# Channel norms in a hybrid decoder layer: sums of split squares on two columns, and factor rows that go through DRAM

## The chip, the cores and the metric

The kernel runs on one core of a Trainium2 chip, as one launch. The metric is the device time of that launch in microseconds (us). The core's engines have one name each here: PE is TensorE (matmuls; PEld are its weight loads), DVE is VectorE, ACT is ScalarE, POOL is GpSimd, SP is SyncE. SP, POOL and ACT each have a queue of transfers.

## What is computed

One decoder layer on 512 tokens of width 1024, all in fp32: a SwiGLU feed-forward network (ffn1), a hybrid mixer (a Mamba-2 scan of four groups and differential attention of eight heads, with one input and one output projection), cross attention into 256 memory tokens, a second feed-forward network (ffn2) and a last norm. The change touches two norms of the mixer. In the attention, the output of each head (128 channels) is normed for each token:

```python
w = p[:, :, 0] - lam * p[:, :, 1]
o = einsum('bhqk,bkhe->bqhe', w, v)          # 8 heads, 128 channels
...
o = o * lax.rsqrt(jnp.mean(o * o, axis=-1, keepdims=True) + EPS)
y_attn = (o * subln_w * (1.0 - lambda_init)).reshape(bsz, seqlen, DA_WIDTH)
```

In the scan, the gated output of each group (256 channels) is normed for each token:

```python
y = y.reshape(bsz, seqlen, SSD_WIDTH) * jax.nn.silu(z)
yg = y.reshape(bsz, seqlen, SSD_GROUPS, SSD_WIDTH // SSD_GROUPS)
yg = yg * lax.rsqrt(jnp.mean(yg * yg, axis=-1, keepdims=True) + EPS)
y_ssd = yg.reshape(bsz, seqlen, SSD_WIDTH) * ssd_norm_w
...
return jnp.concatenate([y_ssd, y_attn], axis=-1) @ w_out
```

## The kernel before

Everything is kept with channels on the 128 partitions and the 512 tokens along the row, so a projection takes its weights in blocks of 128x128 and 512 columns of tokens. Each fp32 matrix is split into a high and a low part of a type with which PE multiplies at full rate (fp32r, called `R32`), and a product is three passes: high by high, high by low, low by high. `split` (with `split_into`, lines 152 to 163) makes the parts: the high part by a copy on ACT (line 155), the low part by a subtraction on DVE (line 156). `mm` (lines 143 to 146) issues a matmul, `transpose` (148 to 150) a transpose on PE. Weights come through three buffers: `wr` is loaded by SP's or POOL's queue and split into `wh` and `wl`.

The stages follow one another on PE: ffn1 up to about 345 us, the mixer up to about 837, cross attention up to about 950, ffn2 to the end. In the mixer the dense work (projections `pq`, `pk`, `pv`, `pxbc`, `pz`, and blocks of the output projection `pm`) runs as one chain of generators, and the work of heads and groups is woven into it by the class `Order`. It counts PE's time as instructions are issued (`od.t`); a head or group is a chain that yields a delay from the table `W`, and its next step is issued into the program when the count has reached that point. The order on PE, DVE and ACT then follows from a scheduler that starts from this program order; POOL's and SP's instructions stay in program order. Accumulators for dense work have four banks of PSUM (`acc`), those of heads and groups four others (`aux`).

**A head** (`head`, from line 756) computes scores (`ps`), exponentials (`ec`), their combination, and transposes them (`pt`, `wt`). Then `po` is the product with `v`, channels on partitions, and `of` its copy in SBUF (line 844, ACT). The norm needs a sum over the channels, which lie on the partitions. The head turns `of` round by four transposes (`ptk`), so that tokens are on the partitions; squares and sums it in four passes of ACT (`junk`, line 852); adds the epsilon term (`ev`, DVE); takes the power −1/2 on POOL (`rr`, line 857); multiplies (`on`, line 859, DVE); and turns the result back by four transposes (`pot`). `ya` is the split of that with the norm's weights; the output projection `out_attn` reads it.

**A group** (`group`) multiplies its two halves by the gate, squares them (`ysq`, lines 1020 and 1022), and sums over the partitions with PE: `pn` takes the squares as weights, in blocks of 128x128, and a column of ones, so that four columns hold the sums with tokens on the partitions. This is an fp32 matmul, and the trace shows it as two records each. `inv_rms_cols` (lines 362 to 368) adds the epsilon (`nv`, DVE, line 365) and takes the power (`ncol`, POOL, line 367). `row_of` (lines 370 to 383) makes of these 128x4 factors a row of 512 on all partitions: it splits the factors (`ch`, `cl`, POOL), multiplies each with the identity matrix (two `ndiag`, POOL), and sums over the partitions with two matmuls (`nrow`). The two halves `y` are multiplied with it (line 1033, DVE) and split (`ys`).

Beside this, a generator sums weight blocks for ffn2 in DRAM all through the mixer (`block_sums_in_dram`, lines 1270 to 1292): SP copies a block (line 1285), and POOL's queue adds another to it by an accumulating transfer (line 1289; `isum`, `wsum`).

## Time and profile before

| what | value |
|---|---|
| time, median of 3 runs | 1294.87 us (1294.66 to 1296.31) |
| profiled execution | 1296.09 us, of which its span 1294.1 |
| PE busy | 1281.5 us, 99% of the span |
| PE weight loads | 1123.7 us, 87% |
| DVE busy | 971.9 us, 75% |
| ACT busy | 707.6 us, 55% |
| POOL busy | 118.0 us, 9% |
| mean share of the DMA engines | 42.2% by the queues that SP feeds, 19.9% by POOL's |

A row of a timeline has the start in us, the busy time in us, the engine, the line, the operation and `out<-in` by the program's names, with the tile's size; `x4` says that four like instructions are put into one row, and a bracket at the end has the idle time before it and what ended it. The busy times of neighbouring matmuls overlap a little, since they are pipelined: how long a burst takes is read from the starts of what stands before and behind it. A row of the windows has the stretch, its length, and the busy time and number of instructions of PE, PEld, DVE, ACT and POOL, then the granted clock, the share of the DMA engines and GB/s. A row of transfers has the KB of one and the median time from its issue to its landing.

### The profile page before, as it was taken

How to read it: one execution, taken by the hardware profiler on the slowest of the kernel's cores; microseconds unless marked ns; L12 is line 12 of the kernel's file. 1: busy time of each engine (PE TensorE's matmuls, PEld its weight loads, DVE VectorE, ACT ScalarE, POOL GpSimd, SP SyncE). 2: the span in 40 equal slices, each digit the busy share in tenths (PEclk: the TensorE clock that was granted, in tenths of full speed). 3: DMA queues.
4: the chain of work that ended last, by engine and by line, in shares of the span. 5: the costliest groups of instructions: out<-in, count | busy, mean ns of one | idle time of the engine just before them, and what ended most of it. 6: DMA issues, size and time to landing. Idle time of an engine off the chain costs nothing.

```text
span 1294.1 us, 20089 instructions
## 1 busy us (share of the span) xinstructions
PE 1281.5 (99%) x7709; PEld 1123.7 (87%) x7709; DVE 971.9 (75%) x1549; ACT 707.6 (55%) x1203; POOL 118.0 (9%) x149
## 2 busy tenths in 40 slices
PE   9999999999999999999999999999999999999997
PEld 7889998998988778877888888889899999989995
DVE  6988898797876686567868696645678868877886
ACT  7545564565654564447644574435466646555554
POOL 1001010001101011101102011020001000000000
PEclk9999999999999999999999999999999999999998
DMA  9368677788875436653476567593249876666662
GB/s 331 101 170 209 187 199 199 226 208 227 272 232 155 131 66 169 224 163 96 107 211 187 151 163 227 193 234 107 66 132 255 210 221 184 191 189 190 180 201 92
DMA packets 69551, 234.75 MB, mean 181 GB/s; under 512 B 8192, under 2 KB 9696, under 8 KB 69104
## 3 DMA queue, kind: packets, MB, share of 16 engines
q1 hardware_dynamic: 53488, 180.91, 42.2%
q0 software_dynamic: 13168, 45.67, 19.9%
q10 hardware_dynamic: 2800, 6.91, 1.7%
q8 instruction: 60, 0.98, 0.3%
q14 instruction: 35, 0.29, 0.1%
HBM read 231.30 MB, written 48.29 MB: 216 GB/s over the span
## 4 chain that ended last, share of the span: by engine, by line
PE 82%; issue 12%; DMA 2%; ACT 1%; DVE 1%; POOL 1%; POOLq 0%; SPq 0%; ACTq 0%
PE qb L243 12%; PE pm L146 10%; PE qe L243 8%; PE qa L243 8%; PE pxbc L146 5%; PE ob L1327 5%; PE oa L1327 4%; PE oe L1327 4%; PE pcq L146 3%; PE pz L146 3%; PE pa L146 2%; PE pk L146 2%; PE pq L146 2%; PE pcv L146 2%; PE pv L146 2%
## 5 line engine op out<-in xcount | busy, mean ns | idle before, releaser
L155 ACT ACTIVATE wh<-wr 128x1024 fp32r<-128x1024 f32 (+1 forms) x245 | 251.2, 1028 | 235.2 <-PE qe L243 27.9
L156 DVE TENSOR_TENSOR wl<-wr,wh 128x1024 fp32r<-128x1024 f32 (+1 forms) x245 | 290.8, 1188 | 83.5 <-ACT wh L155 61.3
L1313 ACT ACTIVATE wh<-wr 128x1024 fp32r<-128x1024 f32 (+1 forms) x78 | 76.9, 987 | 68.4 <-PE ob L1327 19.5
L1315 DVE TENSOR_TENSOR wl<-wr,wh 128x1024 fp32r<-128x1024 f32 (+1 forms) x78 | 87.5, 1131 | 15.0 <-ACT wh L1313 13.1
L789 ACT ACTIVATE ec<-ec,mn 128x512 f32<-128x512 f32 (+3 forms) x64 | 35.4, 554 | 21.9 <-DVE mn L788 21.9
L788 DVE CUSTOM_DVE_ANT_0 ec<-ps,bias 128x512 f32<-128x512 f32 (+3 forms) x64 | 28.1, 486 | 14.8 <-PE ps L146 14.7
L252 POOL DMA_DIRECT2D wr<-in_f2q x11 | 9.7, 881 | 309.8 <-DMA wr<-in_f2q 156.2
L902 DVE SCALAR_TENSOR_TENSOR conv<-pxbc,par,conv 128x511 f32<-128x511 f32 (+2 forms) x48 | 35.7, 745 | 2.3 <-ACT conv L898 1.5
L367 POOL TENSOR_TENSOR ncol<-nv,mhalf 128x4 f32<-128x4 f32 (+1 forms) x9 | 9.7, 1077 | 294.1 <-DVE nv L365 266.5
L146 PE MATMUL pxbc<-hnl,wh 128*128 128x512 f32 x128 | 35.4, 403 | 0.0
L146 PE MATMUL pxbc<-hnh,wh 128*128 128x512 f32 x128 | 35.3, 400 | 0.0
L146 PE MATMUL pxbc<-hnh,wl 128*128 128x512 f32 x128 | 32.3, 393 | 0.0
L454 DVE TENSOR_TENSOR gate<-qb,row 128x512 f32<-128x512 f32 x19 | 13.2, 692 | 22.1 <-PE qb L243 22.1
L146 PEld LDWEIGHTS pxbc<-hnh,wl 128*128 128x128 f32 x128 | 23.8, 188 | 5.3 <-issue 0.3
L252 POOL DMA_DIRECT2D wr<-in_f1q x16 | 14.0, 875 | 152.8 <-DMA wr<-in_f1q 49.8
L146 PEld LDWEIGHTS pxbc<-hnl,wh 128*128 128x128 f32 x128 | 23.3, 188 | 4.8 <-issue 0.4
L146 PEld LDWEIGHTS pxbc<-hnh,wh 128*128 128x128 f32 x128 | 23.2, 189 | 4.5 <-issue 0.3
L455 ACT ACTIVATE gate<-gate 128x1024 f32<-128x1024 f32 x19 | 20.1, 1056 | 10.9 <-DVE gate L454 10.9
L146 PE MATMUL pv<-wh,hnh 128*128 128x512 f32 x64 | 25.3, 395 | 0.0
L146 PE MATMUL pv<-wh,hnl 128*128 128x512 f32 x64 | 25.2, 393 | 0.0
L155 ACT ACTIVATE s24h<-s 128x512 fp32r<-128x512 f32 x30 | 18.8, 627 | 9.0 <-DVE s L214 8.9
L857 POOL TENSOR_TENSOR rr<-ev,mhalf 128x4 f32<-128x4 f32 x8 | 8.3, 1035 | 161.3 <-DVE ev L855 161.3
(465 smaller groups left out, 3546.9 us busy)
## 6 DMA issues: line engine op xcount, KB each, us to landing
wr<-in_f2q SPq DMA_DIRECT2D x44, 512.0 KB, 4.8
wr<-in_f1q SPq DMA_DIRECT2D x40, 512.0 KB, 4.5
wr<-in_f1b SPq DMA_DIRECT2D x23, 512.0 KB, 5.7
isum<-in_f2q SPq DMA_DIRECT2D x22, 512.0 KB, 5.8
wr<-isum SPq DMA_DIRECT2D x22, 512.0 KB, 4.0
wsum<-in_f2b SPq DMA_DIRECT2D x20, 512.0 KB, 6.3
wr<-wsum SPq DMA_DIRECT2D x20, 512.0 KB, 4.7
wr<-in_f1q POOLq DMA_DIRECT2D x16, 512.0 KB, 7.2
```

The source lines that it names most:

```text
L146: newest_mm[:] = [nc.tensor.matmul(out, w, x, start=start, stop=stop).ins]
L155: S.activation(hi, src, AF.Copy),
L156: V.tensor_tensor(lo, src, hi.bitcast(F32), ALU.subtract),
L243: newest_mm[:] = [nc.tensor.matmul(out, w_[:, wc], xs[kp][which][x_], start=first and j == 0 and f == 0 and kp == 0, stop=j == 2 and kp == ...
L252: last_sum[:] = [G.dma_start(raw, m, accum_op=ALU.add).ins]
L455: S.activation(gate, gate, AF.Silu)
L788: V.tensor_tensor_reduce(out=ec[:, :n], in0=ps[c][:, parts[i]], in1=bias[:, T - n :], scale=0.125, scalar=3e38, op0=ALU.add, op1=ALU.min, ...
L789: S.activation(ec[:, :n], ec[:, :n], AF.Exp, bias=mn, scale=-1.0, accum_out=sm[c][:, i : i + 1])
L902: V.scalar_tensor_tensor(y[:, d:], ps[:, : T - d], par[:, cw + j : cw + j + 1], y[:, d:], ALU.mult, ALU.add)
L1313: high = S.activation(hi, raw, AF.Copy)
L1315: low = V.tensor_tensor(lo, raw, hi.bitcast(F32), ALU.subtract)
L1327: newest_mm[:] = [nc.tensor.matmul(ps, a_[:, ts], b_[:, ws], start=first and k == 0 and j == 0, stop=k == n - 1 and j == 2, skip_group_che ...
```

## The change

Six of the eight heads (those with `hd % 4 < 3`: 0, 1, 2, 4, 5 and 6) take a new way, `normed_far`. The square of `of` is taken with channels on partitions (`osq`, ACT) and split into halves (`osqh` on ACT, `osql` on DVE). The sums come from PE as in the groups, with the halves of the squares as weights, but from fp32r matmuls on two columns of ones (`pon`, eight of them). `ev` and `rr` follow on DVE and POOL. The 128x4 factors are then written to DRAM (`there`) and read back on all partitions as a row of 512 (`far`), both by POOL's queue (`row_by_dram`, with the delays `rw` and `rr` of the table); DVE multiplies `of` with the weights and the row (`on`), which is read with a stride of four since the row in DRAM has the four blocks inmost; and `ya` is split from SBUF. The transposes `ptk` and `pot` and the passes `junk` are not done in these heads. Heads 3 and 7 keep the old way.

In all four groups the summed squares are split and `pn` is made of eight fp32r matmuls on two columns. Groups 0, 1 and 2 take `row_by_dram` in place of `row_of`; group 3 keeps `row_of`.

```diff
+W |= {"hn": 4.2, "rw": 8.0, "rr": 12.0}
...
+    def row_by_dram(col, landed, read):
+        there = dram.tile([P, 4], F32, name=nm("there"))
+        G.dma_start(there, col)
+        yield landed
+        row = s2("far")
+        G.dma_start(row, bass.AP(there.tensor, there.offset, [[0, P], [1, 4 * P]]))
+        yield read
+        return row.rearrange("p (t b) -> p b t", b=4)
+
+    def blocks(t):
+        return t.rearrange("p (b t) -> p b t", b=4)
...
         of = s2("of")
         S.activation(of, po, AF.Copy)
+        if hd % 4 < 3:
+            yield from normed_far(hd, of, sm[0])
+            return
         yield W["hv"]
         pt = aux("ptk")
...
+    def normed_far(hd, of, sums):
+        sq = s2("osq")
+        S.activation(sq, of, AF.Square)
+        sq = split("osq", sq)
+        yield W["hn"]
+        pon = aux("pon", (P, 4, 2))
+        for b in range(4):
+            for j in range(2):
+                mm(pon[:, b], sq[j][:, b * P : (b + 1) * P], ones_r[:, 0:2], j == 0, j == 1)
+        ev = small("ev", 4)
+        V.scalar_tensor_tensor(ev, sums, EPS, sums, ALU.mult, ALU.mult)
+        V.scalar_tensor_tensor(ev, pon[:, :, 0], 1.0 / P, ev, ALU.mult, ALU.add)
+        rr = small("rr", 4)
+        G.tensor_tensor(rr, ev, mhalf, ALU.pow)
+        row = yield from row_by_dram(rr, W["rw"], W["rr"])
+        on = s2("on")
+        V.scalar_tensor_tensor(blocks(on), blocks(of), wsub, row, ALU.mult, ALU.mult)
+        ya[hd] = split("ya", backwards(on))
         dump(f"ya_{hd}", ya[hd][0])
...
         V.tensor_tensor(sq[0], sq[0], sq[1], ALU.add)
+        sq = split("ysq", sq[0])
         yield W["gq"] + (1.2 if g == 2 else 0.0)
-        pn = aux("pn", (P, 4))
+        pn = aux("pn", (P, 4, 2))
         for b in range(4):
-            mm(pn[:, b : b + 1], sq[0][:, b * P : (b + 1) * P], ones[:, 0:1], True, True)
-
-        rh = inv_rms_cols(pn, 4, 4.0 / (4 * 256), 4.0 * EPS)
-        yield W["gn"]
-        pr = yield from row_of(rh, 4, G, G, W["gr"])
+            for j in range(2):
+                mm(pn[:, b], sq[j][:, b * P : (b + 1) * P], ones_r[:, 0:2], j == 0, j == 1)
+
+        rh = inv_rms_cols(pn[:, :, 0], 4, 4.0 / (4 * 256), 4.0 * EPS)
+        if g < 3:
+            pr = yield from row_by_dram(rh, W["rw"], W["rr"])
+        else:
+            yield W["gn"]
+            pr = blocks((yield from row_of(rh, 4, G, G, W["gr"])))
         for j in range(2):
             n = 2 * g + j
-            V.scalar_tensor_tensor(yz[j], yz[j], par[:, C_SSD + n : C_SSD + n + 1], pr, ALU.mult, ALU.mult)
+            V.scalar_tensor_tensor(blocks(yz[j]), blocks(yz[j]), par[:, C_SSD + n : C_SSD + n + 1], pr, ALU.mult, ALU.mult)
             ys[n] = split("ys", yz[j])
```

The change moves instructions. On PE in head 1 (the weights of a dense matmul are `wh` or `wl`, here of `pk`; a row names the moving operand first, and the number behind a name tells buffers apart), this stood there before, where a transpose of the head's next weights ends and the dense `pk` runs on:

```order
L150 MATMUL pt_4998<-ident,ec_4872 128x128
L150 MATMUL ptk_5003<-ident,of_4960 128x128 x4
L146 MATMUL pk_4930<-hnl_3919,wh_4933 128x512
L146 MATMUL pk_4930<-hnl_3947,wh_4933 128x512
L146 MATMUL pk_4930<-hnl_3969,wh_4933 128x512
L146 MATMUL pk_4930<-hnl_3999,wh_4933 128x512
L146 MATMUL pk_4930<-hnl_4027,wh_4933 128x512
L146 MATMUL pk_4930<-hnl_4047,wh_4933 128x512
L146 MATMUL pk_4930<-hnh_3870,wl_4934 128x512
L146 MATMUL pk_4930<-hnh_3888,wl_4934 128x512
L146 MATMUL pk_4930<-hnh_3918,wl_4934 128x512
```

And this stands there now, a few matmuls further on:

```order
L147 MATMUL pk_4933<-hnl_4047,wh_4936 128x512
L147 MATMUL pk_4933<-hnh_3870,wl_4937 128x512
L147 MATMUL pk_4933<-hnh_3888,wl_4937 128x512
L147 MATMUL pon_5020<-ones_r,osqh_4967 128x2
L147 MATMUL pon_5020<-ones_r,osql_4968 128x2
L147 MATMUL pon_5020<-ones_r,osqh_4967 128x2
L147 MATMUL pon_5020<-ones_r,osql_4968 128x2
L147 MATMUL pon_5020<-ones_r,osqh_4967 128x2
L147 MATMUL pon_5020<-ones_r,osql_4968 128x2
L147 MATMUL pon_5020<-ones_r,osqh_4967 128x2
L147 MATMUL pon_5020<-ones_r,osql_4968 128x2
L147 MATMUL pk_4933<-hnh_3918,wl_4937 128x512
```

The `ptk` burst behind `pt` is gone, and the `pon` burst stands eight dense matmuls later, behind the first two of the pass with `wl`.

On DVE at group 0 (`wl` are low parts of weights that `pv` and `pq` read, `nv` the epsilon step, `vl` the low part of a finished bank of `pv`), this stood there before:

```order
L365 TENSOR_SCALAR nv_5858<-pn_5853 128x4
L156 TENSOR_TENSOR wl_5970<-wr_5967,wh_5969 128x1024
L156 TENSOR_TENSOR wl_6006<-wr_6003,wh_6005 128x1024
L1033 SCALAR_TENSOR_TENSOR y_5678<-y_5678,par,nrow_5912 128x512
L1033 SCALAR_TENSOR_TENSOR y_5769<-y_5769,par,nrow_5912 128x512
L156 TENSOR_TENSOR ysl_5917<-y_5678,ysh_5916 128x512
L156 TENSOR_TENSOR ysl_5922<-y_5769,ysh_5921 128x512
L156 TENSOR_TENSOR vl_5949<-pv_5791,vh_5948 128x512
```

And this stands there now:

```order
L366 TENSOR_SCALAR nv_5875<-pn_5866 128x4
L157 TENSOR_TENSOR wl_5970<-wr_5967,wh_5969 128x1024
L1074 SCALAR_TENSOR_TENSOR y_5687<-y_5687,par,far_5932 128x512
L1074 SCALAR_TENSOR_TENSOR y_5778<-y_5778,par,far_5932 128x512
L157 TENSOR_TENSOR wl_6005<-wr_6002,wh_6004 128x1024
L157 TENSOR_TENSOR vl_5949<-pv_5804,vh_5948 128x512
```

The two multiplications of `y` now read `far` in place of `nrow`, and stand ahead of one `wl` and of the first `vl`; the low parts `ysl` come later.

On POOL at group 0 (`wsum` are the accumulating transfers), this stood there before:

```order
L367 TENSOR_TENSOR ncol_5860<-nv_5858,mhalf 128x4
L372 CAST ch_5875<-ncol_5860 128x4
L374 TENSOR_TENSOR cl_5877<-ncol_5860,ch_5875 128x4
L378 TENSOR_TENSOR ndiag_5879<-ident,ch_5875 128x512
L378 TENSOR_TENSOR ndiag_5881<-ident,cl_5877 128x512
L1289 DMA wsum_282<-wsum_280 128x512
L1289 DMA wsum_283<-wsum_282 128x1024
```

And this stands there now:

```order
L368 TENSOR_TENSOR ncol_5877<-nv_5875,mhalf 128x4
L373 DMA there_5879<-ncol_5877 128x4
L1330 DMA wsum_282<-wsum_280 128x512
L376 DMA far_5932<-there_5879 128x512
L1330 DMA wsum_283<-wsum_282 128x1024
```

The four operations of the row are gone, and a transfer `there` and a transfer `far` stand on either side of the accumulate into `wsum_282`.

More of the change, by code (lines that the diff above doesn't have):

```diff
@@ L864, in head @@
         ya[hd] = split("ya", backwards(pt), wsub)
+        dump(f"ya_{hd}", ya[hd][0])
+    def normed_far(hd, of, sums):
[16 more added lines that the diff above has]
+        ya[hd] = split("ya", backwards(on))
         dump(f"ya_{hd}", ya[hd][0])
```

## The prediction

> **What bounds the kernel now.** I read the page first, for the span and the busy times.

> ```profile
> span 1294.1 us, 20089 instructions
> PE 1281.5 (99%) x7709; PEld 1123.7 (87%) x7709; DVE 971.9 (75%) x1549; ACT 707.6 (55%) x1203; POOL 118.0 (9%) x149
> ```

> TensorE is busy 99% of the span. The change lies in the mixer alone, so next I asked for TensorE's waits between 400 and 840 us, and for the busy time of each engine from 400 to 500 us.

> ```profile
> PE po L146 <- ACT wt L155: 0.4, 1, 0.4
> PE py L146 <- DVE th L994: 0.2, 1, 0.2
> ...
> 400.00:500.00 100.00, 99.58 (x524) 79.54 (x523) 66.87 (x164) 53.09 (x135) 12.32 (x14) 1.00 0.52 130
> ```

> In 440 us TensorE waits 0.6 us. VectorE works 67 us of 100 there, ScalarE 53, GpSimd 12, and the granted clock is 1.00. So the time is the sum of what is issued on TensorE. An edit pays by the TensorE time that it removes, or costs by a wait that it makes; work on other engines costs only where TensorE is made to wait. The unit comes from the chain of waits.

> ```profile
> 553.63 5.44 PE pq L146 x24
> ```

> A 512-column matmul takes 5.44/24 = 0.2267 us.

> **Heads on TensorE.** Each of six heads loses two bursts of four transposes and gains one of eight two-column matmuls. The old bursts are read from TensorE's timeline in head 0, each between dense matmuls.

> ```profile
> 414.81 0.86 PE L146 MATMUL pq<-hnl,wh 128*128 128x512 f32 x3
> 415.51 0.60 PE L150 MATMUL ptk<-ident,of 128*128 128x128 f32 x4
> 415.87 1.40 PE L146 MATMUL pq<-hnl,wh 128*128 128x512 f32 x5
> 417.11 1.98 PE L146 MATMUL pq<-hnh,wl 128*128 128x512 f32 x8
> ...
> 420.74 1.07 PE L146 MATMUL pk<-hnl,wh 128*128 128x512 f32 x4
> 421.65 0.60 PE L150 MATMUL pot<-ident,on 128*128 128x128 f32 x4
> 422.00 1.18 PE L146 MATMUL pk<-hnl,wh 128*128 128x512 f32 x4
> 423.02 1.77 PE L146 MATMUL pk<-hnh,wl 128*128 128x512 f32 x7
> ```

> From 414.81 to 417.11 are 2.30 us and eight dense matmuls (1.81), so `ptk` adds 0.48 (the difference unrounded). From 420.74 to 423.02 are 2.28, so `pot` adds 0.46. A head loses 0.94.

> No two-column fp32r matmul stands in the trace. Its nearest row is the groups' `pn`: eight matmuls of one column, each with its own 128x128 weights, as the new burst has.

> ```profile
> 539.32 1.30 PE L146 MATMUL pv<-wl,hnh 128*128 128x512 f32 x5
> 540.46 0.95 PE L146 MATMUL pn<-ones,ysq 128*128 128x1 f32 x8
> 541.27 0.96 PE L146 MATMUL pv<-wl,hnh 128*128 128x512 f32 x3
> 542.06 0.40 PE L146 MATMUL pv<-wh,hnh 128*128 128x512 f32 x1
> ```

> From 539.32 to 542.06 are 2.74; less eight dense matmuls, `pn` adds 0.93, or 0.116 per record. That is the pace of its weight loads. Does an fp32r weight load go faster? The loads in the trace say no:

> ```profile
> 412.35 0.19 PEld L146 LDWEIGHTS po<-wt,vh 128*128 128x128 f32 x1 [0.18 <-ACT vh L155]
> 412.45 0.53 PEld L146 LDWEIGHTS po<-wt,vl 128*128 128x128 f32 x3
> ...
> 413.72 0.19 PEld L146 LDWEIGHTS po<-wt,vl 128*128 128x128 f32 x1 [0.21 <-DVE vl L156]
> 413.83 0.59 PEld L146 LDWEIGHTS po<-wt,vh 128*128 128x128 f32 x4
> ```

> These are fp32r weights, after a wait, when nothing holds them back: the second starts 0.10 and 0.11 after the first. So I give the new burst `pn`'s 0.93. A head changes by 0.93 − 0.94 = −0.01, six heads by −0.1. In two heads (0 and 6) the order puts dense matmuls inside the burst; I charge one weight load of 0.1 for each, +0.2. The groups' `pn` keeps eight records, four of fp32 becoming eight of fp32r: 0.

> [...]

> **Groups on TensorE.** Three groups lose the pair of `nrow` matmuls.

> ```profile
> 547.99 0.62 PE L146 MATMUL nrow<-ndiag,ones_r 128*128 128x512 f32 x2
> 548.45 0.40 PE L146 MATMUL pv<-wh,hnh 128*128 128x512 f32 x1
> ...
> 553.47 1.07 PE L146 MATMUL pq<-hnh,wh 128*128 128x512 f32 x4
> ```

> From 547.99 to 548.45 are 0.46; three times that is −1.4. `pq` of head 4, now at 553.47, would come at 553.0.

> **The squares.** The new burst needs `of`, its square, and the square's two halves. Three rows price them, and a fourth shows TensorE at head 1, where `ptk` ahead of it (0.46) is gone as well:

> ```profile
> 451.82 0.60 ACT L844 ACTIVATE of<-po 128x512 f32<-128x512 f32 x1 [1.92 <-PE po L146]
> ...
> L1020 ACT ACTIVATE ysq<-y x8: 611/634/636, 528.3 to 784.5; 128x512 f32<-128x512 f32 x8
> ...
> L156 DVE TENSOR_TENSOR ysl<-y,ysh x8: 682/693/693, 550.4 to 804.1; 128x512 fp32r<-128x512 f32 x8
> ...
> 454.53 1.07 PE L146 MATMUL pk<-hnh,wl 128*128 128x512 f32 x4
> ```

> Ready at 451.82 + 0.60 + 0.63 (square) + 0.63 (high half, a ScalarE pass of the same size) + 0.69 = 454.4. In the new order the burst stands behind the first two of the matmuls that start at 454.53, so at 454.53 + 2 x 0.2267 − 0.46 = 454.5 in the new time. It just fits: 0. VectorE gains 0.69 per head and group and waits at `osql` for ScalarE; behind it are queued the next head's `ec` steps, and PSUM's auxiliary banks cover their delay. At 67 of 100 us busy it can make this up. If that cover is gone, this is the third rival.

> **The way through DRAM.** GpSimd loses the casts and diagonals, and gains two transfers per norm: 128x4 factors to DRAM (`there`), then, once that has landed, 256 KB to all partitions (`far`). The wait for `there` holds GpSimd's own later transfers (the accumulates of weight sums for ffn2, hundreds of us early: 0). What matters is when VectorE gets to the operation that reads `far`. The tightest place is group 0:

> ```profile
> 541.69 1.03 POOL L367 TENSOR_TENSOR ncol<-nv,mhalf 128x4 f32<-128x4 f32 x1 [49.80 <-DVE nv L365]
> ...
> 545.81 1.74 POOL L1289 DMA_DIRECT2D wsum<-wsum  x2
> ```

> ```profile
> 547.79 1.23 DVE L156 TENSOR_TENSOR wl<-wr,wh 128x1024 fp32r<-128x1024 f32 x1 [4.24 <-DMA wr<-in_wq]
> 548.93 1.40 DVE L1033 SCALAR_TENSOR_TENSOR y<-y,par,nrow 128x512 f32<-128x512 f32 x2
> ...
> 551.64 2.00 DVE L156 TENSOR_TENSOR vl<-pv,vh 128x512 fp32r<-128x512 f32 x3
> ```

> ```profile
> bias<-rel_d ACTq DMA_DIRECT2D x8, 256.0 KB, 3.9
> ...
> mem<-in_memT POOLq DMA_DIRECT2D x8, 128.0 KB, 7.1
> ...
> wsum<-wsum POOLq DMA_DIRECT2D x2, 256.0 KB, 5.2
> ...
> cum_d<-ct_sb POOLq DMA_DIRECT2D x1, 32.0 KB, 2.8
> ```

> `there` leaves at 542.7 and lands 2.8 later (the small write to DRAM, `cum_d`), at 545.5. Between the two GpSimd issues a 256 KB accumulate of `wsum`. `far` follows: 3.9 if it moves like the broadcast `bias` (549.4), 7.1 like `mem` (552.6). I take 5.2, that of the accumulate ahead of it in the same queue: 550.7.

> In the new order the two `y` multiplications that read `far` stand ahead of a `wl` and of the `vl` that frees the first bank of `pv`, which `pq` writes. After the landing VectorE needs 1.40 + 1.23 + 0.69 (a third of 2.00, rounded up) = 3.3. So TensorE starts `pq` at 550.7 + 3.3 = 554.0 in place of 553.0: **+1.0**. With 3.9 it is 552.7, no wait (0); with 7.1 it is 555.9 (+2.9). The point from which it costs is a landing at 549.7. That `far` is read with a stride of four elements I price at nothing.

> [...]

> The next tightest place is group 2:

> ```profile
> 755.42 1.03 POOL L367 TENSOR_TENSOR ncol<-nv,mhalf 128x4 f32<-128x4 f32 x1 [40.93 <-DVE nv L365]
> ...
> 767.59 0.42 DVE L977 TENSOR_TENSOR st<-pst,st 128x256 f32<-128x256 f32 x1
> ```

> `far` lands at 756.45 + 2.8 + 5.2 = 764.5 (766.4 with 7.1), and its reader stands behind this `st`, which ends at 768.0: 0. The six heads leave their readers over a head's scores: 0.

> **The sum.** Heads −0.1, split bursts +0.2, `nrow` −1.4, wait at group 0 +1.0: −0.3. The profiled execution took 1296.09 (its span and 2.0 around it) and would take 1295.8. The median of the runs is 1294.87, 1.2 below it; the same step gives **1294.6**. With the wait at 0 or 2.9 the forecast's own range is 1293.5 to 1296.5. A difference of 0.2%, 2.6 us, is about what a measurement here can tell from no change.

> **The rivals.** [...] Chance 0.17.

> (2) Slower: both legs at group 0 queue behind the accumulates on GpSimd's queue, 7.1 each as `mem` shows. `far` lands at 542.7 + 14.2 = 556.9, VectorE frees the bank at 560.2, and TensorE waits 7.2 in place of 1.0: −1.3 + 7.2 = +5.9, 1300.8. It decides from 549.7 on and passes the 2.6 us at a landing of 553.6. For it: `wsum` is on the same queue. Against: `there` has 8 KB and leaves ahead of that accumulate. Chance 0.13.

> (3) Slower: the split squares come late. If VectorE is inside a `wl` (1.23) when ScalarE ends `osqh`, `osql` waits half of that on average, and TensorE with it, since its order is fixed: 6 x 0.61 = +3.7, 1298.3. It decides at head 1 from 454.5 on. For it: no slack there by my sum. Against: in the new order VectorE reaches `osql` before it is ready. Chance 0.10.

> The forecast keeps 0.60; within it, I leave 0.03 for a result under −2.6 us and 0.03 for one over +2.6. That the change does nothing measurable is the forecast itself.

> **The numbers.** Faster: 0.17 + 0.03 = 0.20. Slower: 0.13 + 0.10 + 0.03 = 0.26. Same: 0.54. The range runs from rival 1 with no wait at group 0 (−1.0 more, 1289.7) to rival 3's 1298.3; it leaves out rival 2 and the dearer half of rival 3, 0.18 together.

> **What would show it.** [...] At group 0, `far` landing near 550.7, VectorE idle before `y` by a DMA, and TensorE waiting about 1 us before `pq` (none: the cheaper leg; 7: rival 2). No TensorE wait before `pon` (some 0.6 each: rival 3). TensorE's busy time lower by about 1.3. I would be wrong if dense matmuls after `pon` or a reader of `far` in the heads waited, or if ScalarE, with two more passes in each group, fell behind with `wh`.

## The result, and the profile after

The changed kernel takes 1301.68 us (median of 5 runs, 1300.8 to 1302.5) where the kernel before took 1294.8 on the same chip: a ratio of 1.0051, 95% interval 1.0039 to 1.0062. It is slower by 6.9 us, above the range of the prediction. Timed once more beside other kernels it took 1299.38 (8 runs, 1297.8 to 1301.7), ratio 1.0031 (1.0021 to 1.0041); experiment 11 has what differs between two of these executions.

The page of the profile after, its span and busy times:

```profile
span 1300.4 us, 20080 instructions
PE 1283.3 (99%) x7703; PEld 1123.9 (86%) x7703; DVE 979.2 (75%) x1559; ACT 707.8 (54%) x1171; POOL 122.7 (9%) x155
```

TensorE's share looks the same. That is the average over the whole span; the loss is in one place. TensorE's waits between 400 and 850 us (engine, what waited, what ended it; total, times, longest):

```profile
PE pq L147 <- DVE vl L157: 5.4, 1, 5.4
PE pm L147 <- DVE x L912: 0.6, 1, 0.6
```

Before there were 0.4 and 0.2. The 5.4 us are `pq` of head 4, at the place behind group 0 that the prediction named. GpSimd's timeline there:

```profile
543.39 1.03 POOL L368 TENSOR_TENSOR ncol<-nv,mhalf 128x4 f32<-128x4 f32 x1 [49.10 <-DVE nv L366]
544.72 0.65 POOL L373 DMA_DIRECT2D there<-ncol  x1 [0.30 <-POOL ncol L368]
545.37 0.91 POOL L1330 DMA_DIRECT2D wsum<-wsum  x1
548.48 0.58 POOL L376 DMA_DIRECT2D far<-there  x1 [2.21 <-DMA there<-ncol]
```

The factors are ready at 544.42. From there to the issue of `far`, which waits for `there` to land, are 4.1 us. VectorE's timeline in the same place:

```profile
544.01 1.23 DVE L157 TENSOR_TENSOR wl<-wr,wh 128x1024 fp32r<-128x1024 f32 x1 [0.71 <-PE pv L147]
556.25 2.16 DVE L1074 SCALAR_TENSOR_TENSOR y<-y,par,far 128x512 f32<-128x512 f32 x2 [11.02 <-DMA far<-there]
558.33 1.22 DVE L157 TENSOR_TENSOR wl<-wr,wh 128x1024 fp32r<-128x1024 f32 x1
559.47 0.68 DVE L157 TENSOR_TENSOR vl<-pv,vh 128x512 fp32r<-128x512 f32 x1
```

`far` lands 7.8 us after its issue. VectorE stands idle for 11.0 us until then, with a `wl` and the `vl` that frees the first bank of `pv` queued behind. And TensorE:

```profile
554.22 0.61 PE L147 MATMUL pv<-wl,hnh 128*128 128x512 f32 x2
560.20 3.67 PE L147 MATMUL pq<-hnh,wh 128*128 128x512 f32 x8 [5.37 <-DVE vl L157]
563.71 2.00 PE L147 MATMUL pq<-hnl,wh 128*128 128x512 f32 x8
```

It stops from 554.83 to 560.20. Then the first eight matmuls take 563.71 − 560.20 = 3.51 us, where eight take 8 x 0.2267 = 1.81: another 1.70 lost behind the wait. The windows around the stop tell why (from, to, length; busy time and instructions of PE, PEld, DVE, ACT, POOL; then the granted clock, DMA share, GB/s):

```profile
555.00:556.50 1.50, 0.00 (x0) 0.00 (x0) 0.24 (x1) 1.01 (x2) 0.00 (x0) 1.00 1.02 202
556.50:557.00 0.50, 0.00 (x0) 0.00 (x0) 0.50 (x1) 0.00 (x0) 0.00 (x0) 0.78 1.02 193
557.00:560.00 3.00, 0.00 (x0) 0.00 (x0) 3.00 (x4) 0.00 (x0) 0.00 (x0) 0.50 0.68 164
560.00:563.40 3.40, 3.20 (x8) 2.52 (x9) 3.08 (x5) 0.00 (x0) 0.00 (x0) 0.50 0.50 156
563.40:566.00 2.60, 2.60 (x13) 2.15 (x12) 0.00 (x0) 0.26 (x1) 0.00 (x0) 0.96 1.11 403
```

The granted clock falls to 0.50 at about 556.8, in the middle of the stop (0.78 over half a us is 0.22 us at 0.50), and is back at about 563.6. While TensorE waits that costs nothing; from 560.2 on matmuls start 0.43 us apart in place of 0.23.

Two views answer to the other steps. The transfers of the new way, and the multiplications that read `far` (durations: least, median, most, in ns):

```profile
far<-there POOLq DMA_DIRECT2D x9, 256.0 KB, 7.0
there<-rr POOLq DMA_DIRECT2D x6, 2.0 KB, 1.8
there<-ncol POOLq DMA_DIRECT2D x3, 2.0 KB, 1.8
```

```profile
L1074 DVE SCALAR_TENSOR_TENSOR y<-y,par,far x6: 1118/1132/1172, 556.3 to 781.6; 128x512 f32<-128x512 f32 x6
```

And the new burst in head 1, on TensorE's timeline:

```profile
456.40 0.62 PE L147 MATMUL pk<-hnh,wl 128*128 128x512 f32 x2
456.86 0.17 PE L147 MATMUL pon<-ones_r,osqh 128*128 128x2 f32 x1
456.89 0.25 PE L147 MATMUL pon<-ones_r,osql 128*128 128x2 f32 x1
457.00 0.25 PE L147 MATMUL pon<-ones_r,osqh 128*128 128x2 f32 x1
457.11 0.25 PE L147 MATMUL pon<-ones_r,osql 128*128 128x2 f32 x1
...
457.67 0.71 PE L147 MATMUL pk<-hnh,wl 128*128 128x512 f32 x2
458.23 0.38 PE L151 MATMUL pt<-ident,ec 128*128 128x128 f32 x2
```

From the second on the two-column records start 0.11 apart, and from 456.40 to 458.23 are 1.83 us with four dense matmuls (0.91): the burst costs 0.92. `pn` added 0.93 before, for four fp32 matmuls that the trace shows as eight records; eight fp32r ones stand in their place.

Where the 6.3 us between the two spans lie is read from the starts of the same matmuls in both traces (us):

| stretch | before | after | difference |
|---|---|---|---|
| start to the first `pq` (ffn1) | 368.3 | 370.4 | +2.1 |
| first `pq` to first late `pv` (heads 0 to 2) | 162.0 | 161.6 | −0.4 |
| that `pv` to `pq` of head 4 (group 0) | 23.2 | 28.2 | +5.0 |
| that `pq` to first `pcq` (half clock, rest of the mixer) | 284.2 | 286.0 | +1.8 |
| `pcq` to the last matmul (cross attention, ffn2) | 446.8 | 446.3 | −0.5 |
| from there to the end of the span | 9.7 | 8.0 | −1.7 |

Group 0 and the clock behind it give +6.8. The +2.1 in ffn1, where both programs hold the same instructions in the same order, and the −1.7 at the end are not of the change's own work; experiments 9 to 14 take them up.

### The profile page after: what moved, and what is told of

Read it like the earlier page. It is cut to its first block, busy times and chain, and to the rows that moved or that the text cites. A ratio compares the mean times of both kernels' runs of the same rounds, so it can differ in the third digit from the quotient of the medians.

```text
span 1300.4 us, 20080 instructions
## 1 busy us (share of the span) xinstructions
PE 1283.3 (99%) x7703; PEld 1123.9 (86%) x7703; DVE 979.2 (75%) x1559; ACT 707.8 (54%) x1171; POOL 122.7 (9%) x155
## 4 chain that ended last, share of the span: by engine, by line
PE 55%; DVE 1%; ACT 0%; issue 0%; POOLq 0%; POOL 0%; ACTq 0%
PE pm L147 8%; PE qb L244 7%; PE pxbc L147 5%; PE qe L244 5%; PE qa L244 5%; PE pcq L147 3%; PE ob L1368 3%; PE pz L147 3%; PE oa L1368 2%; PE oe L1368 2%; PE pq L147 2%; PE pk L147 2%; PE pcv L147 2%; PE pcs L147 1%; PE pco L147 1%; PE ps L147 1%
## 5 line engine op out<-in xcount | busy, mean ns | idle before, releaser
L156 ACT ACTIVATE wh<-wr 128x1024 fp32r<-128x1024 f32 (+1 forms) x245 | 251.3, 1028 | 250.4 <-issue 29.1
L156 ACT ACTIVATE s24h<-s 128x512 fp32r<-128x512 f32 x30 | 18.8, 626 | 10.6 <-DVE s L215 10.5
L147 PE MATMUL pq<-hnh,wh 128*128 128x512 f32 x64 | 18.6, 425 | 5.4 <-DVE vl L157 5.4
```

Source lines behind the costliest of these rows:

```text
L147: newest_mm[:] = [nc.tensor.matmul(out, w, x, start=start, stop=stop).ins]
L156: S.activation(hi, src, AF.Copy),
```

## The experiments

**1. Group 0 back to the row made by matmuls.**

```diff
-        if g < 3:
+        if 0 < g < 3:
             pr = yield from row_by_dram(rh, W["rw"], W["rr"])
```

> Group 0 alone goes back to the row made by matmuls (row_of); everything else as changed. Theory A (the loss is one place: VectorE stands at group 0's multiplication until far lands, TensorE stops 5.4 us before pq and then runs eight matmuls at half clock, 1.7 us): 5.4 + 1.7 go, 0.46 for nrow comes back, so 6.6 below the changed kernel's 1301.7: about 1295. TensorE has no wait over 1 us at pq. Rival B (the loss is spread: two more passes on VectorE and ScalarE, more DMA traffic, dense work that runs late): at most half of it goes, 1298 or more.

1293.38 us (11 runs; ratio to before 0.9985, 0.9977 to 0.9994), 8.3 under the changed kernel. TensorE's waits in the mixer:

```profile
PE pm L147 <- DVE x L912: 0.6, 1, 0.6
```

The wait at `pq` is gone, and with it the half clock (1.00 from 545 to 570 us). The whole loss goes with one of nine round trips. Rival B, that it is spread, falls. The gain is 8.3 where 6.6 was expected, and the table above has a reason: the first `pq` stands at 368.4 here, so the 2 us that ffn1 took longer in the changed kernel's first profile are not in this run. It is also 1.6 faster than the kernel before, since the end of its span is 8.0 as in the changed kernel, and not 9.7.

**2. Group 0 through DRAM, its two multiplications later on VectorE.**

```diff
+        ready = list(last) if g == 0 else []
         for j in range(2):
             n = 2 * g + j
-            V.scalar_tensor_tensor(blocks(yz[j]), ...)
+            with behind(ready):
+                V.scalar_tensor_tensor(blocks(yz[j]), ...)
```

> Group 0 keeps the way through DRAM and its transfers, but its two multiplications are put behind the next finished split on VectorE (the low part of q, some 6 us later), so that the low parts of v don't queue behind them. Theory A: no TensorE wait at pq and no clock drop; all of 5.4 + 1.7 goes and nrow stays out: 1301.7 - 7.1 = about 1294.6, 0.4 under the run with group 0's old row. Rival B: 1298 or more. Rival C (the transfers themselves hold the weights' loads up, so that TensorE waits at pq or pk whatever VectorE's order is): a wait of several us on wh or wl of wq or wk remains, 1297 to 1300.

1292.97 us (11 runs; ratio 0.9983, 0.9974 to 0.9992). No wait at `pq`, though `there`, the accumulate and `far` are issued as before. VectorE's timeline:

```profile
548.82 0.69 DVE L157 TENSOR_TENSOR vl<-pv,vh 128x512 fp32r<-128x512 f32 x1 [0.71 <-ACT vh L156]
...
558.90 0.68 DVE L161 SCALAR_TENSOR_TENSOR ql<-pq,qh 128x512 fp32r<-128x512 f32 x1
559.51 2.18 DVE L1076 SCALAR_TENSOR_TENSOR y<-y,par,far 128x512 f32<-128x512 f32 x2
```

`vl` now runs when `pv` is done, and the multiplications start without a wait. So the transfers did not hold TensorE up themselves (C falls); the place of their reader in VectorE's order, ahead of `vl`, did, with the landing as late as it was.

**3 and 4. The heads alone, and the groups alone.**

```diff
-        if g < 3:
+        if g < 0:
             pr = yield from row_by_dram(rh, W["rw"], W["rr"])
```

> The six heads as changed; all groups make their row with matmuls (the split squares stay in the groups' pn). Theory A: the heads are neutral, since the fp32r burst costs as much TensorE time as the two transposes that it replaces (0.91 + about 0.3 for the two split bursts in all, against 0.94 per head): before's 1294.8 within 1. Rival B: the split squares and the far reads of the heads cost several us by themselves: 1297 or more.

```diff
-        if hd % 4 < 3:
+        if hd % 4 < 0:
             yield from normed_far(hd, of, sm[0])
```

> The groups as changed; all eight heads keep their transposes. Theory A: the whole loss is here: before's 1294.8 + 5.4 + 1.7 - 3 x 0.46 = about 1300.5, with the TensorE wait of about 5 us at pq and the granted clock at 0.5 behind it. Rival B: about half of the 6.9 us, 1297 to 1298.5.

Heads alone: 1296.78 (11 runs; ratio 1.0014, 1.0005 to 1.0023), 1.8 over before. Groups alone: 1302.65 (5 runs; 1.0057, 1.0044 to 1.0069), with the wait in the profile:

```profile
PE pq L147 <- DVE vl L157: 4.2, 1, 4.2
```

The loss is the groups'. The heads cost a little: from the first `pq` to `pcq` 470.1 us in place of 469.3, and 0.9 more at the end of the span. Counted from the first `pq` they are 0.3 under before up to 750 us; 1.1 us are lost between 750 and 775, around group 2, where blocks of the output projection stand at other places. Runs 2 and 8, whose groups go through DRAM, lose 0.8 us in the same place. What does it there was not tried.

**5. `far` ahead of the accumulate.**

```diff
-            pr = yield from row_by_dram(rh, W["rw"], W["rr"])
+            pr = yield from row_by_dram(rh, 2.0 if g == 0 else W["rw"], W["rr"] + (6.0 if g == 0 else 0.0))
```

> As changed, but at group 0 GpSimd issues far right behind there, ahead of the 256 KB accumulate of wsum. Theory A1 (the two legs are long in themselves: 1.8 to 3.7 for there, 6.2 and more for far on GpSimd's queue): far still lands about 10 us after ncol; the wait at pq shrinks by at most 2 (5.4 to 3.5 to 5), and the time is 1299 to 1301.5. Theory A2 (both legs stand behind the accumulate): there lands in 1.8, far in about 6, 4 us sooner; the wait falls to about 1.5 and, with it, the clock drop goes: about 1295.5.

1298.78 us (10 runs; ratio 1.0026, 1.0017 to 1.0035). GpSimd's and VectorE's timelines:

```profile
542.94 0.65 POOL L373 DMA_DIRECT2D there<-ncol  x1 [0.30 <-POOL ncol L368]
547.13 0.58 POOL L376 DMA_DIRECT2D far<-there  x1 [3.55 <-ACT wh L156]
547.70 1.78 POOL L1330 DMA_DIRECT2D wsum<-wsum  x2
```

```profile
552.96 2.18 DVE L1074 SCALAR_TENSOR_TENSOR y<-y,par,far 128x512 f32<-128x512 f32 x2 [9.50 <-DMA far<-there]
```

With nothing between them on this queue, it is still 4.2 from the issue of `there` to the issue of `far` (3.6 to the landing, 0.6 behind it), and `far` takes 5.8. The wait is 3.9 and the clock falls. That is A1's picture; A2, the accumulate in between, falls, the more so since the changed kernel's second profile (11) has the same 5.8 with the accumulate ahead. The time itself is level with the second set of the changed kernel (1299.38): the intervals of the two ratios overlap.

**6. `far` by ScalarE's queue.**

```diff
-        G.dma_start(row, bass.AP(there.tensor, ...))
+        (by or G).dma_start(row, bass.AP(there.tensor, ...))     # by = S for group 0
```

> As changed, but group 0's far goes by ScalarE's queue, whose broadcast of the same 256 KB (bias) takes 3.9 to 5.7 us; there stays on GpSimd's queue. Theory A1 (GpSimd's queue is slow for this broadcast): far lands 2 to 3.5 us sooner, the wait at pq falls from 5.4 to 2 to 3.4; if the clock drops only after a longer wait, its 1.7 us go as well: 1296.5 to 1298.5. Rival (the broadcast of one DRAM row to 128 partitions is slow on any queue): 6 to 7 us again and 1300 or more. ScalarE stands at the transfer until there has landed; wh of wq is split behind it, which may cost up to 2 us of its own.

1301.86 us (4 runs; ratio 1.0051, 1.0037 to 1.0064). ScalarE's and VectorE's timelines:

```profile
547.15 0.33 ACTq L376 DMA_DIRECT2D far<-there  x1
```

```profile
556.32 2.15 DVE L1074 SCALAR_TENSOR_TENSOR y<-y,par,far 128x512 f32<-128x512 f32 x2 [11.79 <-DMA far<-there]
```

9.2 us, longer than by GpSimd's queue, and a wait of 6.1. So another queue does not make it fast; it is no clean test of the queue, though, since two accumulates (256 and 512 KB) had been issued ahead of `far` here, and one in the changed kernel. The DMA engines were busy all this time (shares of 1.00 to 1.10 from 548 to 556, as in the first windows of the stop above). The first profile of the changed kernel shows other transfers slow in this place too: against the same ones in the kernel before, the 256 KB accumulate took 8.3 us in place of 5.6, the load of `wq`'s weights by SP's queue 6.0 in place of 4.2, `bias` by ScalarE's queue 5.7 in place of 3.9. So transfers of three queues took longer in this place than before; no run isolates why.

**7. `far` read without the stride.** The factors lie in another order then, so that the norm of a token takes another token's factor.

```diff
-        return row.rearrange("p (t b) -> p b t", b=4)
+        return blocks(row)
```

> As changed, but far is read in the order in which it lies, without the stride of four (the factors then belong to other tokens: the norm is applied wrongly). Theory: the twelve multiplications that read it take 0.70 us in place of 1.13; at group 0 the wait at pq shrinks by 2 x 0.43 = 0.9 to about 4.5, the clock drop stays, and the time is 0.9 lower: about 1300.8. [...]

1298.68 us (6 runs; ratio 1.0027, 1.0016 to 1.0038). VectorE's timeline:

```profile
554.01 1.41 DVE L1074 SCALAR_TENSOR_TENSOR y<-y,par,far 128x512 f32<-128x512 f32 x2 [10.57 <-DMA far<-there]
```

1.41 for two in place of 2.16: the stride costs 0.38 per multiplication, so 0.8 of the wait. The time alone does not show it: it is 3.0 under the first set of the changed kernel and 0.7 under the second (1299.38), whose ratio's interval overlaps with this one's.

**8. Heads as before, groups as changed, group 0 as in 2** (the edits of 2 and 4 together).

> Heads as before the change, groups as changed, with group 0's two multiplications behind the low part of q. Theory A (heads neutral, three nrow pairs saved): before's 1295.0 - 1.4 = 1293.6, within 1 of the run with heads changed too (1293.0). Rival (the heads' new way saves TensorE time that shows once the wait is gone): 1294.5 or more.

1295.29 us (11 runs; ratio 1.0000, 0.9991 to 1.0009). By the time alone the rival holds. The trace says otherwise: from the first `pq` to `pcq` it takes 468.8 us, in run 2 468.5, before 469.3. What differs is the end of the span, 10.1 us from the last burst of matmuls in place of 8.0.

**9 and 12. More instructions on GpSimd.** In the traces GpSimd's last drain is long exactly where the end is late: 6.6 us in the kernel before, 3.6 in the changed one. Two runs add 24 small memsets to its program in the cross attention, to the kernel before and to the kernel of 8.

```diff
+        if hd == 0:
+            for _ in range(24):
+                G.memset(small("fill", 4), 0.0)
         es = [None, None]
```

> The kernel before, with 24 small memsets of an unused tile added to GpSimd's program in the cross attention, where it idles. In the profiles so far GpSimd's last drain takes 6.6 to 7.5 us in the kernels with none, three or six round trips through DRAM and 3.5 in those with eight or nine, and the span ends 1.7 to 2.6 us later behind the last transfer. Theory T (this hangs on how long GpSimd's program is, not on the round trips): the drain falls to about 3.5 and the time by 1.7, to 1293.3. Rival (it hangs on something that the round trips do): drain 6.6, time as before, 1295.0.

> Heads as before the change, groups as changed with group 0's multiplications put behind, and the 24 memsets on GpSimd in the cross attention. Theory T: the end is 2.1 us shorter than in the same kernel without the memsets (1295.3), so 1293.2, level with the run that had the heads changed too (1293.0): the heads bring nothing. Rival (the memsets do nothing to the end): 1295.3.

1294.94 us (11 runs; ratio 1.0000, 0.9992 to 1.0009) and 1295.12 (11 runs; 0.9999, 0.9990 to 1.0007), with drains of 6.6 and 7.1 us as without the memsets. The theory falls: 24 more instructions leave the drain and the time as they were.

**13 and 14. More transfers on GpSimd's queue.** 18 small writes are added to the kernel before, 12 to the kernel of 8, so that each has the 18 transfers of nine round trips.

```diff
+        fill = small("fill", 4)
+        G.memset(fill, 0.0)
+        for _ in range(5 if hd < 2 else 4):        # range(3) in the other
+            G.dma_start(dram.tile([P, 4], F32, name=nm("spare")), fill)
         es = [None, None]
```

> The kernel before, with 18 small writes to DRAM (128x4, of an unused tile) on GpSimd's queue in the cross attention; as many transfers as nine round trips have. GpSimd's last drain took 6.6, 7.1 and 7.5 us in kernels with 0, 6 and 12 transfers more than before, and 3.5 in those with 16 and 18; 24 memsets did nothing to it. Theory N (the end hangs on the number of transfers on GpSimd's queue): drain 3.5 and 1293.3. Rival (it hangs on something else in which the kernels differ): drain 6.6 or more, 1295.1.

> Heads as before the change, groups as changed with group 0's multiplications put behind (1295.3 before this edit), and 12 more small writes on GpSimd's queue, 18 transfers more than before in all. Theory N: drain 3.5, 2.1 less: 1293.2. Rival: drain 7.1, 1295.3.

1294.10 us (11 runs; ratio 0.9986, 0.9977 to 0.9994) and 1292.69 (12 runs; 0.9979, 0.9970 to 0.9987). The drains, from the traces:

| transfers on GpSimd's queue | kernels | GpSimd's last drain, us |
|---|---|---|
| 100 | before, 9 | 6.6 |
| 106 | 4, 8, 12 | 7.1 |
| 112 | 3 | 7.5 |
| 116 to 118 | changed, 1, 2, 5, 6, 7, 10, 11, 13, 14 | 3.5 to 3.7 |

Theory N holds: writes that nobody reads make the kernel before 1.2 faster and the kernel of 8 by 2.6. What in the queue makes this count matter was not tried. So 1.7 us of the changed kernel's time are saved by chance of a count, and what its norms cost is 1.7 more than the difference of the times. The kernel of 14, with the heads as they were, is the fastest of the study, level with 2 (1292.97): the heads' new way brings nothing.

**10. A shorter wait.** As 5, with only one of the two multiplications ahead of the low parts of `v`.

```diff
+            with behind(list(last) if g == 0 and j == 0 else []):
                 V.scalar_tensor_tensor(blocks(yz[j]), ...)
```

> As the run with far ahead of the accumulate, but only one of group 0's two multiplications stays ahead of the low parts of v; the other goes behind the low part of q. The wait at pq should fall from 3.9 by one multiplication, to about 2.8. Theory K1 (the granted clock falls only when TensorE idles for longer than some 3 us): clock 1.00 throughout, eight matmuls of pq in 1.81 us, time 1298.8 - 1.1 - 1.6 = 1296.1. Theory K2 (any stop of over 2 us costs the clock): clock 0.5 behind it, 1297.7.

1297.66 us (10 runs; ratio 1.0017, 1.0008 to 1.0027), K2's figure. TensorE, and the windows of the stop:

```profile
555.14 3.58 PE L147 MATMUL pq<-hnh,wh 128*128 128x512 f32 x8 [3.30 <-DVE vl L157]
558.56 2.00 PE L147 MATMUL pq<-hnl,wh 128*128 128x512 f32 x8
```

```profile
554.50:555.00 0.50, 0.00 (x0) 0.00 (x0) 0.50 (x1) 0.00 (x0) 0.24 (x1) 0.93 0.57 201
555.00:558.50 3.50, 3.36 (x8) 2.68 (x9) 3.02 (x5) 0.00 (x0) 0.56 (x1) 0.52 0.88 229
558.50:560.00 1.50, 1.50 (x8) 1.19 (x8) 0.00 (x0) 0.00 (x0) 0.00 (x0) 1.00 1.02 310
```

The wait was 3.3, since `far` took 6.6, and so not as short as meant. The clock fell all the same, from 554.9 to 558.3, and cost 3.42 − 1.81 = 1.6. This run alone does not exclude K1, with a wait of 3.3 and a limit of 3 us; the changed kernel's first profile is against it, since there the clock fell when the stop had lasted 1.95 us. K2 is not shown for stops shorter than 3.3.

**11. The changed kernel again** (no edit).

> The changed kernel again, for a second profile of it. Its first profile was 2.0 us later than before's at the first pq of the mixer already, in ffn1, where both programs hold the same instructions in the same order. If that is one execution's chance, the second profile has it near 368.3 and the median is near 1300; if it belongs to this build, it is near 370.4 again and the median near 1301.7. Both theories of the cause: a wait at pq of 4 to 5.5 us and the clock at 0.5 behind it.

1299.38 us, between the two. Its profile has the first `pq` at 367.8, so the +2.1 of ffn1 belonged to that execution. GpSimd, VectorE and TensorE:

```profile
546.14 0.58 POOL L376 DMA_DIRECT2D far<-there  x1 [2.44 <-ACT wh L156]
```

```profile
551.95 2.19 DVE L1074 SCALAR_TENSOR_TENSOR y<-y,par,far 128x512 f32<-128x512 f32 x2 [9.29 <-DMA far<-there]
```

```profile
555.92 3.58 PE L147 MATMUL pq<-hnh,wh 128*128 128x512 f32 x8 [3.67 <-DVE vl L157]
559.34 2.02 PE L147 MATMUL pq<-hnl,wh 128*128 128x512 f32 x8
```

`far` took 5.8 here and 7.8 in the first profile; the wait is 3.7 in place of 5.4, the clock costs 1.6. The same kernel's loss at group 0 moves with how long `far` takes from one execution to the next. That is part of why its runs spread over 4.7 us, from 1297.8 to 1302.5: the two executions with a profile are the fastest and the slowest of them, and their spans differ by 4.4, of which 1.7 lie at group 0 and 2.6 in ffn1. Why ffn1 took longer is open.

## Why the prediction was wrong

The place was right, and the chain through it: `ncol`, `there`, `far`, the multiplications, `wl`, `vl`, `pq`, with the stop beginning from a landing at 549.7 on. The step that failed is the term "**+1.0**" for the wait at group 0. It was too small by three things:

- **The two legs.** The prediction took 2.8 for `there` and 5.2 for `far`, 8.0 from the end of `ncol`. The first profile shows 4.1 and 7.8, 11.8 in all: 3.8 more. (The second: 10.1.) Of the 3.8, 0.9 are issue time that the sum left out (0.3 from `ncol` to the issue of `there`, 0.6 from its landing to the issue of `far`), 0.4 are `there` (3.2 to its landing) and 2.6 `far`. The row that came nearest was `mem`, 7.1 for half the bytes on the same queue, which stood in the prediction as the dear end; the median of the nine `far` is 7.0. The accumulate was nearest in queue and size, but its 5.2 did not hold in this place even for an accumulate, which took 8.3.
- **The stride**, "priced at nothing", makes two multiplications 2.16 in place of 1.40: 0.8 more.
- **The clock.** 1.0 + 3.8 + 0.8 = 5.6 us of wait, measured 5.4. Behind it TensorE ran at half clock until 563.6, which cost 1.7 and stood nowhere in the sum. The prediction read the granted clock, 1.00 in the mixer, and never asked what a stop would do to it.

So the term was 5.4 + 1.7 = 7.1 in place of 1.0. Runs 1 and 2 show that all of it hangs on this one wait. The prediction's own dear end, +2.9 with `mem`'s 7.1, would not have reached it: it too lacked the issue time, the stride and the clock.

The other steps, in the prediction's order:

- **Heads on TensorE**, −0.1 and +0.2 for the split bursts: the burst costs 0.92 against 0.93 forecast. Counted from the first `pq`, the heads alone (run 3) are 0.3 under before at 750 us, behind all eight heads, where +0.1 was forecast. The 0.8 over before that they show at `pcq` arises around group 2 and is open.
- **`nrow`**, −0.46 each: from `pv` to `pq`, run 2 takes 22.7 where before took 23.2, and run 8 gains another 0.5 at group 1. Right for these two. What the third gives can't be read, since 0.8 is lost around group 2: at `pcq`, runs 2 and 8 are 0.8 and 0.5 under before, where the sum without the wait has −1.3.
- **The squares**, 0: no wait of TensorE before `pon` in the list of waits. Right, and rival 3 falls.
- **The other readers of `far`**, 0: none of them shows in TensorE's waits, though `far` took 7.0. Right; `pm` waits 0.6 for a VectorE step in the kernels with groups through DRAM, which the prediction had not.
- **Rival 1**, faster weight loads, gives the range its lower end of 1289.7 and has 0.17 of the chances. No run shows such a load: the records of `pon` start 0.11 apart, and the burst costs 0.92. It falls.
- **Rival 2** gave 1300.8 at a chance of 0.13. Its time is close, but its mechanism, both legs behind the accumulates of the queue, is not what run 5 shows, and its wait of 7.2 is in truth 5.4 and a clock. (`there` has 2 KB by the list of transfers, not the 8 KB that the rival's text gives it.)

What the prediction could not have had in its sum is the end of the program, 1.7 less by the count of transfers. It made the result look better than the wait is.

## What to carry to other kernels

When a step is moved through DRAM, take both legs from the dearest row of the same kind on the same queue, add the issue time around them, and then ask what stands behind the reader on its engine: eight round trips, with `far` taking up to 9.7 us, made TensorE wait nowhere, and one cost everything. A stop of TensorE of some us is to be priced with the half clock behind it, 1.6 to 2.8 us in the seven profiles here, so that a wait has a step in its cost and not only a slope. The shortest of these stops was 3.3 us; one of 0.9, at 315.8 us in the changed kernel's first profile, cost no clock (1.00 there). Nothing is shown for what lies between. And before a gain of 1 or 2 us is believed, compare the starts of the same matmuls stage by stage; two of the terms here, +2.1 and −1.7, had nothing to do with the edit.

## What the runs showed of the hardware

**The granted clock at a stop of TensorE.** In seven profiles with a stop at `pq`, the clock records of the traces give these stretches of 0.50:

| run | idle from | to | half clock from | to | length |
|---|---|---|---|---|---|
| changed | 554.8 | 560.2 | 556.8 | 563.6 | 6.83 |
| 4 | 553.1 | 557.4 | 557.5 | 560.9 | 3.41 |
| 5 | 553.1 | 556.9 | 556.7 | 560.1 | 3.41 |
| 6 | 554.1 | 560.3 | 559.1 | 566.0 | 6.83 |
| 7 | 553.0 | 557.2 | 555.5 | 562.4 | 6.83 |
| 10 | 551.8 | 555.1 | 554.9 | 558.3 | 3.41 |
| 11 | 552.3 | 555.9 | 555.7 | 559.1 | 3.41 |

**The end of this program hangs on the number of transfers on GpSimd's queue**: its last drain grows from 6.6 to 7.5 us between 100 and 112 transfers and is 3.5 to 3.7 at 116 to 118. The span behind the last matmul is shorter by less than the drain is, 8.0 us in place of 9.7 to 10.5. Runs 13 and 14, which add only such transfers and one memset, show it; why it is so is open.
